# Pool groups of a hybrid decoder block: windows of 8 and 16 by a running sum, the window of 2 by one difference

## The chip, the cores and the metric

The kernel runs on one core of one Trainium2 chip. Time is device microseconds of one execution; before the change three runs took 1905.4, 1900.44 and 1904.27 us, a median of 1904.27. The profile is of one further execution. The engines are named as in the profile: PE is TensorE (PEld its weight loads), DVE is VectorE, ACT is ScalarE, POOL is GpSimd, SP is SyncE, which here issues most DMAs. Each engine works through its own queue in order; an instruction that has to wait holds up all that stand behind it on that engine.

## The reference

One decoder layer on 2048 tokens of 1024 features, all in float32:

```
h = x + W_out( concat[ RMSNorm(PoolMix(u_pool)), RMSNorm(StickBreakAttn(q, k, v)) ] )
    with [u_pool | q | k | v] = RMSNorm(x) @ W_in
h = h + W_down( relu(RMSNorm(h) @ W_up) ** 2 )
y = RMSNorm(h)
```

The change is in the pool mixer. It has four groups of 128 channels with windows of 2, 4, 8 and 16 tokens:

```python
for g, w in enumerate(POOL_WINDOWS):          # 2, 4, 8, 16
    xg = ug[:, :, g, :]
    cs = jnp.cumsum(xg, axis=1)
    cs_lag = jnp.pad(cs, ((0, 0), (w, 0), (0, 0)))[:, :S]
    count = jnp.minimum(pos + 1, w)
    outs.append((cs - cs_lag) / count - xg)   # mean of the last w tokens, less the token
mapped = jnp.einsum('bsgc,gcd->bsgd', pooled, pool_w)
y = mapped.reshape(B, S, D_POOL) * pool_scale
```

## The kernel before

Features lie on the 128 partitions and tokens along the free dimension, in four tiles of 512 tokens (j = 0 to 3). Every float32 product is made of three matmuls on a high and a low part: `split` (L145, L146) lets ACT copy the high part and DVE subtract it for the low part. That pair of lines serves the weights (`hl`), the normalized input (`h`), the attention tiles (`at`), the queries and keys (`qk`) and the pool tiles (`pls`).

The program has a front, an output projection, and two feed-forward stages. In the front the tiles go through the input projection in two pairs (0 and 1, then 2 and 3). A projection group is 24 matmuls (L177 to L179) into one of two PSUM banks, `pd`, and then an evacuation: `pool_group` for column groups 0 to 3, `keep_qk` and `keep_v` for the others. Weights are split `WAHEAD = 5` halves of a group ahead. Tiles 0 and 2 take their pool groups after six other groups, tile 1 takes them first and tile 3 last. In between, pieces of the attention are put in: logits `pz` (L630, L631), a scan of products on DVE (L663), transposes `pta` (L677), a split into `at`, and the products with the values, `po` (L689), summed at L648 (`ot`).

`pool_group(j, g, ps)` takes the projected group from PSUM into `u` (ACT L394, for tile 0 DVE L392), with the last `PAD` = 15 tokens of the tile before in front of it (POOL, L390 and L395). The sum over the window is made by doubling: at L400 an add of the tile to itself shifted by 1, then 2, 4 and 8 tokens, so one add for the window of 2 and four for that of 16. L403 makes `pl`, the sum times 1/w less `u`; in tile 0, L405 and L406 correct the first w - 1 tokens with a table of reciprocals. `pl` is split into `pls`, three matmuls with the pool's weights `pw` follow (L410 to L412, into `pp`), and ACT scales the result (L413). `pool_weights` loads these weights (L296) and splits them.

The order on each engine is set by a scheduler, which plans the whole program with estimated durations when the kernel is built. So a change of one stage's instructions also moves others against each other on all engines.

Of the kernel before, what the change touches and what calls it, by code (L numbers as in the profile page):

```python
# [8 lines left out]
F32 = mybir.dt.float32  # L9
# [4 lines left out]
ALU = mybir.AluOpType  # L14

P = 128
S = 2048
D = 1024
T = 512
NT = S // T  # L20
# [8 lines left out]
WARM = 9  # L29
SCRATCH = 2048  # L30
WINDOWS = (2, 4, 8, 16)
PAD = 15
EPS = 1e-6
RATIO_FRONT = (0.3, 0.4, 0.15, 0.4, 0.4, 0.3)
RATIO_TAIL = 0.6
# [10 lines left out]
def hymba_block(ctx: ExitStack, tc: tile.TileContext, xT, gains, w_in, pool_w, w_out, w_up, w_down, out):  # L46
    nc = tc.nc
# [3 lines left out]
    const = pool("const", 1)  # L51
# [55 lines left out]
    for n in (D, D // 2):  # L107
        inv[n] = const.tile([P, 1], F32, name=f"inv{n}")
        nc.vector.memset(inv[n], 1.0 / n)
    recip = const.tile([P, PAD], F32, name="recip")  # L110
    for i in range(PAD):
        nc.vector.memset(recip[:, i:i + 1], 1.0 / (i + 1))
# [9 lines left out]
    yrlast = const.tile([P, 2, 2, TB], F32R, name="yrlast")  # L122
    carry = const.tile([P, len(WINDOWS), PAD], F32, name="carry")
    nc.vector.memset(carry, 0.0)


    qs = [[dram.tile([P, T], F32R, name=f"qs{h}_{j}") for j in range(NT)] for h in range(H)]
# [14 lines left out]
    def split(dst, src):  # L142

        hi, lo = dst
        nc.scalar.activation(hi, src, AF.Copy)  # L145
        return nc.vector.tensor_tensor(lo, src, hi.bitcast(F32), ALU.subtract)  # L146
# [147 lines left out]
    def pool_weights():  # L294
        raw = pa.tile([P, PAD + T], F32, tag="s", name="pw_raw")[:, 0:4 * P].rearrange("p (g c) -> p g c", g=4)
        nc.sync.dma_start(raw, pool_w)  # L296
        pw.append(pa.tile([P, 2, 4, P], F32R, name="pw", bufs=1))
        split((pw[0][:, 0], pw[0][:, 1]), raw)

# [85 lines left out]
    def pool_group(j, g, ps):  # L385
        w = WINDOWS[g]
        if g == 0:
            st[j]["y"] = pa.tile([P, 4, T], F32, tag="yb", name="yb", bufs=1)
        u = pa.tile([P, PAD + T], F32, tag="u", name="u")
        nc.gpsimd.tensor_copy(u[:, 0:PAD], carry[:, g])  # L390
        if j == 0:
            took = nc.vector.tensor_tensor(u[:, PAD:], ps, st[0]["r"], ALU.mult)  # L392
        else:
            took = nc.scalar.activation(u[:, PAD:], ps, AF.Copy)  # L394
        nc.gpsimd.tensor_copy(carry[:, g], u[:, T:T + PAD])  # L395
        cur, lag = u, 1
        while lag < w:
            nxt = pa.tile([P, PAD + T], F32, tag="s", name="s")
            lo = 2 * lag - 1
            nc.vector.tensor_tensor(nxt[:, lo:], cur[:, lo:], cur[:, lo - lag:PAD + T - lag], ALU.add)  # L400
            cur, lag = nxt, 2 * lag
        pl = pa.tile([P, T], F32, tag="ev", name="pl")
        nc.vector.scalar_tensor_tensor(pl, cur[:, PAD:], 1.0 / w, u[:, PAD:], op0=ALU.mult, op1=ALU.subtract)  # L403
        if j == 0:
            nc.vector.tensor_tensor(pl[:, 0:w - 1], cur[:, PAD:PAD + w - 1], recip[:, 0:w - 1], ALU.mult)  # L405
            nc.vector.tensor_tensor(pl[:, 0:w - 1], pl[:, 0:w - 1], u[:, PAD:PAD + w - 1], ALU.subtract)  # L406
        d = pa.tile([P, 2, T], F32R, tag="st", name="pls", align_bytes=256, bufs=3)
        split((d[:, 0], d[:, 1]), pl)
        pp = psx.tile([P, T], F32, tag="px", name="pp")
        nc.tensor.matmul(pp, pw[0][:, 0, g], d[:, 0], start=True, stop=False)  # L410
        nc.tensor.matmul(pp, pw[0][:, 0, g], d[:, 1], start=False, stop=False)
        nc.tensor.matmul(pp, pw[0][:, 1, g], d[:, 0], start=False, stop=True)  # L412
        nc.scalar.activation(st[j]["y"][:, g], pp, AF.Copy, scale=gs[:, g:g + 1])  # L413
        return took
# [47 lines left out]
    def in_proj(j, c, again=False):  # L462
        if not again:
            wlist.append(w_in[c])
        if c < 4:
            evac = lambda ps: pool_group(j, c, ps)
        elif c < 12:
            evac = lambda ps: keep_qk(j, c % 4, qs if c < 8 else ks, ps)
        else:
            evac = lambda ps: keep_v(j, c - 12, ps)  # L470
# [37 lines left out]
    def front(q):  # L508
# [7 lines left out]
        if q == 0:  # L516
            note(start)
            note(norm1_first)
            note(pool_weights)
        else:  # L520
            note(lambda: (load_x(b, bigp), norm1_rms(b), norm1(b), pace(2)))
# [1072 lines left out]
    pa = inner.enter_context(tc.tile_pool(name="pa", bufs=2))  # L1594
# [70 lines left out]
```

## Time and profile before

| | |
|---|---|
| median of three runs | 1904.27 us (1900.44 to 1905.4) |
| the profiled execution | 1902.05 us, its span 1900.3 us |
| mean granted TensorE clock | 0.995 |
| instructions | 26640 |
| VectorE busy from 0 to 600 us | 477.48 us |
| TensorE busy from 0 to 600 us | 586.35 us |

The front and the output projection take about the first 600 to 700 us. A row of windows gives the busy time of each engine in a stretch and the TensorE clock that was granted there. A row of waits says which engine and line waited for which, how long in total, how often, and the longest. A row of the timeline has start, length, engine, line and operation, and in brackets how long the engine had stood idle and what ended that. Matmuls are pipelined: their lengths overlap, and what counts is the distance from start to start.

### The profile page before, as it was taken

What the parts mean: (1) busy time and instruction counts of PE and PEld (TensorE: products, weight loads), DVE (VectorE), ACT (ScalarE), POOL (GpSimd) and SP (SyncE); (2) the same over time, 40 slices, a digit from 0 to 9 for tenths busy, and PEclk for the clock granted to TensorE, in tenths of its full rate; (3) what the DMA queues carried; (4) which work ended last, traced back from release to release, by engine and by line L of the source; (5) the groups of instructions that cost most, each with busy time, mean ns of one, the idle gap of its engine ahead of it and who ended that gap; (6) DMA issues with size and microseconds to landing.
All of it is one profiled execution on the core that took longest, in us unless ns stands there. A gap on an engine that the chain in (4) does not pass through costs nothing.

```text
span 1900.3 us, 26640 instructions
## 1 busy us (share of the span) xinstructions
PE 1868.9 (98%) x8883; PEld 1554.3 (82%) x8883; DVE 1481.2 (78%) x2151; ACT 1025.2 (54%) x1616; POOL 238.5 (13%) x463
## 2 busy tenths in 40 slices
PE   9999999999999999999999999999999999999997
PEld 7788788788888888777888888887888888888886
DVE  6887789678866886778799988786666677988774
ACT  6565567455644465554567555554332665656543
POOL 0233234122321050000000000000010010020120
PEclk9999999999999999999999999999999999999998
DMA  7676596699888777787899888889999899999852
GB/s 226 212 255 201 177 313 224 194 322 315 281 310 312 278 252 254 284 303 274 307 358 328 303 308 281 298 284 333 388 313 330 281 317 307 332 294 341 289 206 91
DMA packets 222164, 535.91 MB, mean 282 GB/s; under 512 B 26048, under 2 KB 32192, under 8 KB 218176
## 3 DMA queue, kind: packets, MB, share of 16 engines
q1 hardware_dynamic: 217264, 525.46, 79.4%
q0 software_dynamic: 4608, 8.39, 2.4%
q8 instruction: 72, 1.18, 0.3%
q14 instruction: 76, 0.62, 0.1%
q10 hardware_dynamic: 144, 0.26, 0.0%
HBM read 349.46 MB, written 184.55 MB: 281 GB/s over the span
## 4 chain that ended last, share of the span: by engine, by line
PE 50%; DMA 5%; DVE 2%; issue 1%; ACT 1%; POOL 0%; SPq 0%; DVEq 0%; ACTq 0%
PE pb L1291 14%; PE pY L1118 13%; PE pb L1468 12%; PE pZ L1118 7%; PE pX L1118 3%; DMA ar<-sd 1%; DMA hn<-hs 1%; DMA ar<-sdi 1%; PE pb L1408 1%; DMA td<-t 0%; DMA t<-in_w_down_dram 0%; DMA b<-in_w_down_dram 0%; DMA wr<-in_w_down_dram 0%; DVE ad L146 0%; DVE hw L146 0%
## 5 line engine op out<-in xcount | busy, mean ns | idle before, releaser
L1118 PE MATMUL pY<-sa,hw 128*128 128x512 f32 x1536 | 366.3, 390 | 1.9 <-ACT u L1041 1.9
L1118 PEld LDWEIGHTS pY<-sa,hw 128*128 128x128 f32 x1536 | 287.9, 188 | 63.0 <-ACT u L1041 3.4
L1291 PE MATMUL pb<-ad,wd 128*128 128x512 f32 x1344 | 305.4, 389 | 0.7 <-DVE ad L146 0.7
L177 PE MATMUL pd<-h,hl 128*128 128x512 f32 x752 | 297.9, 396 | 1.5 <-DVE qk L146 1.3
L178 PE MATMUL pd<-h,hl 128*128 128x512 f32 x752 | 297.0, 395 | 0.3 <-DVE h L146 0.3
L179 PE MATMUL pd<-h,hl 128*128 128x512 f32 x752 | 297.3, 395 | 0.0
L1291 PEld LDWEIGHTS pb<-ad,wd 128*128 128x128 f32 x1344 | 252.1, 188 | 53.8 <-DVE ad L146 1.5
L1468 PE MATMUL pb<-ad,wd 128*128 128x512 f32 x1104 | 253.9, 390 | 0.9 <-ACT ad L145 0.9
L1468 PEld LDWEIGHTS pb<-ad,wd 128*128 128x128 f32 x1104 | 206.5, 188 | 44.6 <-ACT ad L145 1.3
L146 DVE TENSOR_TENSOR ad<-ar,ad 128x1024 fp32r<-128x1024 f32 x160 | 194.1, 1221 | 44.1 <-ACT ad L145 43.5
L145 ACT ACTIVATE ad<-ar 128x1024 fp32r<-128x1024 f32 x160 | 168.4, 1054 | 95.7 <-PE pb L1468 31.9
L1118 PE MATMUL pZ<-sa,hw 128*128 128x512 f32 x768 | 186.8, 390 | 1.7 <-DVE a L1061 1.7
L1118 PEld LDWEIGHTS pZ<-sa,hw 128*128 128x128 f32 x768 | 143.9, 188 | 32.7 <-DVE a L1061 3.0
L145 ACT ACTIVATE hl<-raw 128x512 fp32r<-128x512 f32 x168 | 104.1, 629 | 115.6 <-PE pd L179 76.7
L177 PEld LDWEIGHTS pd<-h,hl 128*128 128x128 f32 x752 | 142.2, 189 | 29.0 <-DVE qk L146 1.8
L179 PEld LDWEIGHTS pd<-h,hl 128*128 128x128 f32 x752 | 142.0, 189 | 28.2 <-DVE hl L146 0.5
L178 PEld LDWEIGHTS pd<-h,hl 128*128 128x128 f32 x752 | 142.2, 189 | 27.1 <-DVE h L146 0.7
L146 DVE TENSOR_TENSOR hl<-raw,hl 128x512 fp32r<-128x512 f32 x168 | 115.1, 690 | 46.9 <-ACT hl L145 46.5
L1035 ACT ACTIVATE a<-a 128x512 f32<-128x512 f32 x96 | 60.1, 629 | 89.6 <-DVE a L1077 38.5
L146 DVE TENSOR_TENSOR hw<-rt,hw 128x512 fp32r<-128x512 f32 x128 | 86.5, 686 | 25.2 <-ACT hw L145 25.1
L145 ACT ACTIVATE wd<-wq 128x1024 fp32r<-128x1024 f32 x56 | 59.4, 1060 | 77.1 <-PE pb L1291 68.4
L146 DVE TENSOR_TENSOR wd<-wq,wd 128x1024 fp32r<-128x1024 f32 x56 | 68.5, 1222 | 34.3 <-ACT wd L145 32.8
(218 smaller groups left out, 2737.3 us busy)
## 6 DMA issues: line engine op xcount, KB each, us to landing
ar<-sd SPq DMA_DIRECT2D x96, 512.0 KB, 5.9
ar<-sdi SPq DMA_DIRECT2D x64, 512.0 KB, 5.6
rb<-in_w_up_dram SPq DMA_DIRECT2D x30, 1024.0 KB, 6.2
sd<-a SPq DMA_DIRECT2D x104, 256.0 KB, 5.2
raw<-in_w_in_dram SPq DMA_DIRECT2D x50, 512.0 KB, 4.6
sdi<-hr SPq DMA_DIRECT2D x96, 256.0 KB, 5.4
wr<-in_w_down_dram SPq DMA_DIRECT2D x48, 512.0 KB, 5.7
sd<-s SPq DMA_DIRECT2D x88, 256.0 KB, 4.9
```

Of the source, the lines that this page charges most:

```text
L145: nc.scalar.activation(hi, src, AF.Copy)
L146: return nc.vector.tensor_tensor(lo, src, hi.bitcast(F32), ALU.subtract)
L177: nc.tensor.matmul(ps, hl[:, 0, c], hi, start=(k == 0), stop=False)
L178: nc.tensor.matmul(ps, hl[:, 0, c], lo, start=False, stop=False)
L179: last_mm[0] = nc.tensor.matmul(ps, hl[:, 1, c], hi, start=False, stop=(k == n - 1))
L1035: nc.scalar.activation(t, src, AF.Relu)
L1118: nc.tensor.matmul(t, w[:, wx, c], a[:, ax, c % 2], start=first and c == 0 and x == 0, stop=last and c == G - 1 and x == 2, skip_group_che ...
L1291: nc.tensor.matmul(b, t[:, wx, 2 * (kk % 2) + c, i * P:(i + 1) * P], a[:, ax, c], start=p in ("P1", "P5", "P2") and kk == 0 and c == 0 and ...
L1408: nc.tensor.matmul(b[:, cols], block(t, wx, c, n), a[:, ax, c, cols], start=False, stop=(i == 1 and c == 1 and x == 2), skip_group_check=True)
L1468: nc.tensor.matmul(ps[q, n], block(t, wx, c, n), left_[q][:, ax, c], start=(n_ in ("P1", "P3") and kk == 0 and c == 0 and x == 0), stop=(n ...
```

## The change

For the window of 2, `pl` becomes the token before less the token, one subtraction; the factor 1/2 is put on that group's weights when they are loaded (L299 of the changed kernel, before the split). The first token of the sequence is set to zero. For the window of 4 there are two adds as before, over fewer columns. For 8 and 16 one scan adds the incoming token and subtracts the one that leaves the window, starting from `window_sum`, the sum of the last w tokens of the tile before, which a reduce makes after the scan (not in the last tile). The padding becomes 16 tokens, so that the token leaving a window of 16 is at hand.

```diff
-PAD = 15
+PAD = 16
...
+    window_sum = const.tile([P, len(WINDOWS)], F32, name="window_sum")
+    nc.vector.memset(window_sum, 0.0)
...
         nc.sync.dma_start(raw, pool_w)
+        nc.vector.tensor_scalar(raw[:, 0], raw[:, 0], 1.0 / WINDOWS[0], None, op0=ALU.mult)
...
         nc.gpsimd.tensor_copy(carry[:, g], u[:, T:T + PAD])
-        cur, lag = u, 1
-        while lag < w:
-            nxt = pa.tile([P, PAD + T], F32, tag="s", name="s")
-            lo = 2 * lag - 1
-            nc.vector.tensor_tensor(nxt[:, lo:], cur[:, lo:], cur[:, lo - lag:PAD + T - lag], ALU.add)
-            cur, lag = nxt, 2 * lag
         pl = pa.tile([P, T], F32, tag="ev", name="pl")
-        nc.vector.scalar_tensor_tensor(pl, cur[:, PAD:], 1.0 / w, u[:, PAD:], op0=ALU.mult, op1=ALU.subtract)
-        if j == 0:
-            nc.vector.tensor_tensor(pl[:, 0:w - 1], cur[:, PAD:PAD + w - 1], recip[:, 0:w - 1], ALU.mult)
-            nc.vector.tensor_tensor(pl[:, 0:w - 1], pl[:, 0:w - 1], u[:, PAD:PAD + w - 1], ALU.subtract)
+        if w == 2:
+            nc.vector.tensor_tensor(pl, u[:, PAD - 1:PAD + T - 1], u[:, PAD:], ALU.subtract)
+            if j == 0:
+                nc.vector.tensor_tensor(pl[:, 0:1], u[:, PAD:PAD + 1], u[:, PAD:PAD + 1], ALU.subtract)
+        else:
+            sums = pa.tile([P, PAD + T], F32, tag="s", name="s")
+            if w == 4:
+                pair = pa.tile([P, PAD + T], F32, tag="s", name="s")
+                nc.vector.tensor_tensor(pair[:, PAD - 2:], u[:, PAD - 2:], u[:, PAD - 3:PAD + T - 1], ALU.add)
+                nc.vector.tensor_tensor(sums[:, PAD:], pair[:, PAD:], pair[:, PAD - 2:PAD + T - 2], ALU.add)
+            else:
+                nc.vector.tensor_tensor_scan(sums[:, PAD:], u[:, PAD:], u[:, PAD - w:PAD + T - w], window_sum[:, g:g + 1],
+                                             op0=ALU.add, op1=ALU.subtract)
+                if j < NT - 1:
+                    nc.vector.tensor_reduce(window_sum[:, g:g + 1], u[:, PAD + T - w:], axis=mybir.AxisListType.X, op=ALU.add)
+            nc.vector.scalar_tensor_tensor(pl, sums[:, PAD:], 1.0 / w, u[:, PAD:], op0=ALU.mult, op1=ALU.subtract)
...
```

In tile 0 the correction by reciprocals stays for the windows of 4, 8 and 16. The scheduler plans the program anew; the number and kind of PE's instructions stay the same, and from the end of the output projection on the order is the one of before on every engine.

Two places of the new order follow. Rows give the line, operation and operands. In the order a scan is printed as SCALAR_TENSOR_TENSOR. Line numbers are of the kernel that the rows belong to: L148 and L675 of the changed kernel are L146 and L663 of the one before.

The first is tile 1, DVE's queue up to the low part of `pls` of the window of 16. Before:

```order
L400 TENSOR_TENSOR s<-s 128x520
L146 TENSOR_TENSOR hl<-raw,hl 128x512
L663 SCALAR_TENSOR_TENSOR pc<-sh,later_keys 128x512
L648 TENSOR_TENSOR ot<-ot,po 64x512
L400 TENSOR_TENSOR s<-s 128x512
L672 TENSOR_TENSOR sg<-sg,pc 128x2x255
L740 TENSOR_SCALAR zero<-left_137 128x16
L146 TENSOR_TENSOR at<-pta,at 128x384
L146 TENSOR_TENSOR hl<-raw,hl 128x512
L403 SCALAR_TENSOR_TENSOR pl<-s,u 128x512
L741 TENSOR_REDUCE zall<-zero 128x1
L146 TENSOR_TENSOR pls<-pl,pls 128x512
```

The same place with the change:

```order
L660 TENSOR_TENSOR ot<-ot,po 64x512
L414 TENSOR_REDUCE window_sum<-u 128x1
L415 SCALAR_TENSOR_TENSOR pl<-s,u 128x512
L148 TENSOR_TENSOR h<-nt,h 128x512
L148 TENSOR_TENSOR at<-pta,at 128x512
L148 TENSOR_TENSOR h<-nt,h 128x512
L680 TENSOR_TENSOR sg<-sg,pc 128x127
L680 TENSOR_TENSOR sg<-sg,pc 128x255
L148 TENSOR_TENSOR hl<-raw,hl 128x512
L148 TENSOR_TENSOR h<-nt,h 128x512
L148 TENSOR_TENSOR pls<-pl,pls 128x512
```

The last scan of the attention's tile 0 (L663), its product `sg` of 2x255 and the `at` of 384 columns stood ahead of `pls` before; with the change they stand behind it.

On PE, the same pool group's first matmul (L410, with the change L422) stood behind the transposes of an attention unit. Before:

```order
L179 MATMUL pd<-h,hl 128x512
L677 MATMUL pta<-ident,sg 128x128 x3
L177 MATMUL pd<-h,hl 128x512
L178 MATMUL pd<-h,hl 128x512
L179 MATMUL pd<-h,hl 128x512
L410 MATMUL pp<-pls,pw 128x512
```

With the change:

```order
L701 MATMUL po<-at,vw 128x128
L422 MATMUL pp<-pls,pw 128x512
L643 MATMUL pz<-kw,qb 128x256
L642 MATMUL pz<-kw,qa 128x256
L701 MATMUL po<-at,vw 64x128
```

It has moved up, ahead of these transposes and into the products of an earlier unit.

The second place is tile 2, DVE's queue around the `pl` of the window of 16. Before:

```order
L146 TENSOR_TENSOR at<-pta,at 128x512
L400 TENSOR_TENSOR s<-s 128x520
L146 TENSOR_TENSOR hl<-raw,hl 128x512
L663 SCALAR_TENSOR_TENSOR pc<-sh,later_keys 128x512
L400 TENSOR_TENSOR s<-s 128x512
L672 TENSOR_TENSOR sg<-sg,pc 128x2x255
L146 TENSOR_TENSOR at<-pta,at 128x512
L403 SCALAR_TENSOR_TENSOR pl<-s,u 128x512
L648 TENSOR_TENSOR ot<-ot,po 64x512
```

With the change:

```order
L675 SCALAR_TENSOR_TENSOR pc<-sh,later_keys 128x512
L414 TENSOR_REDUCE window_sum<-u 128x1
L415 SCALAR_TENSOR_TENSOR pl<-s,u 128x512
L148 TENSOR_TENSOR pls<-pl,pls 128x512
L148 TENSOR_TENSOR at<-pta,at 128x512
L191 TENSOR_TENSOR ss<-ss,sq 128x512
L684 TENSOR_TENSOR sg<-sg,pc 128x2x255
L675 SCALAR_TENSOR_TENSOR pc<-sh,later_keys 128x512
L660 TENSOR_TENSOR ot<-ot,po 64x512
```

The adds between the attention's rows are gone, and `pl` has moved ahead of the `at` rows that follow it. In the start of the program, the row `L299 TENSOR_SCALAR pw_raw<-pw_raw 128x128` comes in between the last two `h` rows of the first tile on DVE.

More of the change, by code (lines that the diff above doesn't have):

```diff
@@ L395, in pool_group @@
         nc.gpsimd.tensor_copy(carry[:, g], u[:, T:T + PAD])
-        cur, lag = u, 1
-        while lag < w:
-            nxt = pa.tile([P, PAD + T], F32, tag="s", name="s")
-            lo = 2 * lag - 1
-            nc.vector.tensor_tensor(nxt[:, lo:], cur[:, lo:], cur[:, lo - lag:PAD + T - lag], ALU.add)
-            cur, lag = nxt, 2 * lag
-        pl = pa.tile([P, T], F32, tag="ev", name="pl")
-        nc.vector.scalar_tensor_tensor(pl, cur[:, PAD:], 1.0 / w, u[:, PAD:], op0=ALU.mult, op1=ALU.subtract)
-        if j == 0:
-            nc.vector.tensor_tensor(pl[:, 0:w - 1], cur[:, PAD:PAD + w - 1], recip[:, 0:w - 1], ALU.mult)
-            nc.vector.tensor_tensor(pl[:, 0:w - 1], pl[:, 0:w - 1], u[:, PAD:PAD + w - 1], ALU.subtract)
+        pl = pa.tile([P, T], F32, tag="ev", name="pl")
+        if w == 2:
[14 more added lines that the diff above has]
+            nc.vector.scalar_tensor_tensor(pl, sums[:, PAD:], 1.0 / w, u[:, PAD:], op0=ALU.mult, op1=ALU.subtract)
+            if j == 0:
+                nc.vector.tensor_tensor(pl[:, 0:w - 1], sums[:, PAD:PAD + w - 1], recip[:, 0:w - 1], ALU.mult)
+                nc.vector.tensor_tensor(pl[:, 0:w - 1], pl[:, 0:w - 1], u[:, PAD:PAD + w - 1], ALU.subtract)
         d = pa.tile([P, 2, T], F32R, tag="st", name="pls", align_bytes=256, bufs=3)
```

## The prediction

> **What bounds the kernel now.** First the engine table of the page:
>
> ```profile
> span 1900.3 us, 26640 instructions
> PE 1868.9 (98%) x8883; PEld 1554.3 (82%) x8883; DVE 1481.2 (78%) x2151; ACT 1025.2 (54%) x1616; POOL 238.5 (13%) x463
> ```
>
> TensorE (PE) is busy for all but 31 us. The change takes nothing from PE, so shorter VectorE (DVE) work is worth only what PE loses by waiting for it. The windows show where. Columns: window and length, then busy us (instructions) of PE, weight load, DVE, ACT and POOL, granted clock, DMA share, GB/s.
>
> ```profile
> 200.00:210.00 10.00, 6.36 (x38) 5.11 (x36) 9.62 (x19) 4.24 (x8) 4.84 (x3) 1.00 0.69 224
> 210.00:220.00 10.00, 9.43 (x34) 7.43 (x35) 5.79 (x10) 5.37 (x11) 0.00 (x0) 0.83 0.61 150
> 330.00:340.00 10.00, 7.83 (x48) 6.26 (x47) 10.00 (x16) 6.12 (x11) 6.46 (x4) 1.00 0.25 87
> 340.00:350.00 10.00, 9.34 (x38) 7.73 (x39) 8.29 (x13) 4.97 (x9) 0.79 (x3) 0.66 0.65 176
> 50.00:100.00 50.00, 48.99 (x236) 40.00 (x235) 44.41 (x81) 27.93 (x50) 11.42 (x27) 1.00 0.66 217
> 100.00:150.00 50.00, 48.70 (x294) 41.83 (x293) 43.46 (x69) 32.55 (x63) 19.09 (x33) 1.00 0.79 251
> ```
>
> Two places stand out, each a hole in PE followed by a lowered clock, with DVE full ahead of it. The list of waits (for whom: us, times, longest) and the timeline (start, length) say what PE waited for. Place A, token tile 1:
>
> ```profile
> PE pp L410 <- ACT pls L145: 4.0, 1, 4.0
> 205.97 0.40 PE L179 MATMUL pd<-h,hl 128*128 128x512 f32 x1
> 206.44 0.67 DVE L400 TENSOR_TENSOR s<-s 128x512 f32<-128x512 f32 x1
> 208.95 0.68 DVE L403 SCALAR_TENSOR_TENSOR pl<-s,u 128x512 f32<-128x512 f32 x1
> 209.66 0.63 ACT L145 ACTIVATE pls<-pl 128x512 fp32r<-128x512 f32 x1 [2.63 <-DVE pl L403]
> 210.35 0.50 PE L410 MATMUL pp<-pls,pw 128*128 128x512 f32 x1 [3.98 <-ACT pls L145]
> 212.09 0.63 PE L177 MATMUL pd<-h,hl 128*128 128x512 f32 x1
> 212.52 0.63 PE L178 MATMUL pd<-h,hl 128*128 128x512 f32 x1
> 214.47 0.40 PE L177 MATMUL pd<-h,hl 128*128 128x512 f32 x1
> 214.70 0.40 PE L178 MATMUL pd<-h,hl 128*128 128x512 f32 x1
> ```
>
> The pool matmul of the window of 16 stands in PE's queue for a `pl` that DVE makes only at 208.95, behind its fourth doubling add. Afterwards matmuls start 0.43 us apart (212.09, 212.52) instead of 0.23 (214.47, 214.70). Place B, tile 2:
>
> ```profile
> PE pta L677 <- DVE at L146: 1.9, 1, 1.9
> 337.95 0.65 DVE L400 TENSOR_TENSOR s<-s 128x512 f32<-128x512 f32 x1
> 339.14 0.67 DVE L146 TENSOR_TENSOR at<-pta,at 128x512 fp32r<-128x512 f32 x1
> 339.74 0.67 DVE L403 SCALAR_TENSOR_TENSOR pl<-s,u 128x512 f32<-128x512 f32 x1
> ```
>
> Here PE waits for an attention tile `at`, which stands in DVE's queue behind the doubling adds of the same pool group.
>
> **What the two places cost.** From the windows, hole plus clock: A is 10 - 6.36 = 3.64, 10 - 9.43 = 0.57 and (1 - 0.83) x 10 = 1.7, together 5.9 us. B is 2.17 + 0.66 + 3.4 = 6.2 us. Sum **12.1 us**.
>
> **The change part by part.** Prices of DVE operations, from the groups by line and shape (busy, mean ns):
>
> ```profile
> L400 DVE TENSOR_TENSOR s<-u 128x526 f32<-128x526 f32 x16 | 11.2, 697 | 3.6 <-ACT u L394 3.6
> L400 DVE TENSOR_TENSOR s<-s 128x524 f32<-128x524 f32 x12 | 8.3, 692 | 0.1
> L400 DVE TENSOR_TENSOR s<-s 128x520 f32<-128x520 f32 x8 | 5.5, 693 | 0.1
> L400 DVE TENSOR_TENSOR s<-s 128x512 f32<-128x512 f32 x4 | 2.7, 670 | 0.0
> L663 DVE TENSOR_TENSOR_SCAN pc<-sh,later_keys 128x512 f32<-128x512 f32 x56 | 68.6, 1226 | 0.7 <-ACT sh L636 0.7
> L741 DVE TENSOR_REDUCE zall<-zero 128x1 f32<-128x16 f32 x1 | 0.2, 158 | 0.0
> ```
>
> Window 2: add and scaled difference become one difference, 0.69 us less. Window 4: two adds stay, nothing. Window 8: three adds (2.08) become a scan and a small reduce (1.23 + 0.16), 0.69 less. Window 16: four adds (2.75) become the same pair, 1.36 less. That is 2.74 us a tile, 11 us over four tiles; tile 3 has no reduce (0.3 more), tile 0 loses one tiny operation. The scan of add and subtract on two f32 streams is not in the trace. Bounds: 0.69 (a plain add) and 2.45 (twice the nearest scan); I take the row, 1.23.
>
> [...]
>
> What matters more is where the rows now stand. At A, PE's queue holds 109 matmuls between the first pool matmul of window 4 and that of window 16 before, 87 now: with 0.227 us for 512 columns (214.70 - 214.47), half of it for 256, 0.085 for 128 and 0.12 for a transpose, 20.6 and 16.8 us, so PE asks 3.8 us earlier. In DVE's queue, between the second half of window 4's `pls` and the `pl` of window 16, stand 41 rows before (27.9 us) and 23 now (16.4 us), at 0.69 us a 512-wide operation, 0.75 for the six `nt`, 1.23 a scan, and less for narrower rows: ready 11.5 us earlier. The margin grows by 7.7 us and the wait is 4.0: it goes. At B the same count gives 119 against 90 matmuls (19.1, 15.4 us) and 26 against 13 DVE rows (20.0, 9.5 us), a margin better by 6.8 us; the `at` rows lose the adds ahead of them. Were the scan 2.45 us, 2.4 more would stand at each place and both waits would still go. What is late next: attention rows that the pool rows have passed at A (`at`, `sg`, the L663 scan). Each costs PE nothing as long as DVE, full from 190 to 210 before, has its 7.7 us.
>
> Added cost: the scaling of `pw_raw` enters DVE's queue between the third and the fourth of these four rows, and waits there for a DMA.
>
> ```profile
> 8.14 0.33 SPq L296 DMA_DIRECT2D pw_raw<-in_pool_w_dram  x1
> DMA to landing us min/median/max: 5.4/5.4/5.4
> 12.05 2.74 DVE L354 SCALAR_TENSOR_TENSOR h<-xt,gains,h 128x512 fp32r<-128x512 f32 x4
> 17.86 0.62 PE L482 MATMUL pd<-h,hl 128*128 128x512 f32 x2
> ```
>
> It lands at 13.5, DVE comes there at 14.1; the last `h` behind it is used only after 17.86, over 3 us of cover. Its own time, between 0.16 (the reduce) and 0.69 us (a 128x512 operation), is hidden there too; nothing is charged. If the load came over 4 us late, PE would stand for the excess.
>
> Sum against the profiled execution (1902.05 us): 1902.05 - 12.1 = 1890.0. That execution lies 2.2 below the median of the runs, 1904.27, which gives 1892.2 by the same step; I say **1891**.
>
> **The rivals.**
> *One stall stays, or half of each.* PE comes to B about 6 us earlier than before while DVE is still full there (10.00 of 10). Then some 6 us are gained: 1896 to 1898. The granted clock bears on this: B shows that single waits of 1.87 us, close together, already brought the clock down (0.66). [...]
>
> *No net change.* The pool matmuls were moved up with the sums; if the 23 DVE rows wait for inputs rather than run back to back, PE meets the same hole in another row: 1902 to 1904. Against it, DVE was 9.62 and 10.00 busy, so rows removed do count.
>
> *Slower.* The stage after (output projection) gets its weights just in time:
>
> ```profile
> ACT hl L145 <- DMA raw<-in_w_out_dram: 16.6, 6, 5.4
> ```
>
> Weights are split five halves ahead, 5 x 12 x 0.227 = 13.6 us of matmuls. A load is up to 5.4 late now, so 8.2 more can be borne. If those transfers do not move up when PE does (12.1 us), PE stands 3.9 us, the clock falls, and again at the next tiles: the gain is lost, and three bouts at 3.4 us (B) end at 1902 + 10.2 = 1912. It decides once loads land over 13.6 us late. Against: the loads are issued as buffers come free, which happens earlier too.
>
> **How the numbers follow.** Forecast 0.60, one stall left 0.17, no net change 0.14, slower 0.09. About 0.3% (5.7 us: below 1898.6 or above 1910.0) is what a measurement can tell from none. Faster: nearly all of the first and most of the second, 0.73; slower 0.08; same 0.19. Range: downward, the holes of 1.0 and 1.3 us at 50 to 150 may go too, and 1888 less some scatter (the runs span 5 us) is 1885; upward through the second rival to 1901, leaving out about 0.2.
>
> **What would show it.** Right: PE busy 10.00 and clock 1.00 in tile 1's and tile 2's pool stretch, no PE wait on `pls` over 1 us, a scan near 1.23 us, DVE about 11 us less busy. Wrong: another PE wait over 2 us with a clock under 1.00 between 50 and 600; a scan over 2.4 us; PE waiting on `hl` after 490.

## The result and the profile after

| | median us | lowest to highest | runs |
|---|---|---|---|
| before | 1902.41 | 1900.44 to 1905.4 | 4 |
| changed | 1888.08 | 1887.35 to 1889.65 | 4 |

The ratio is 0.9922, with an interval of 0.9909 to 0.9934: 14.3 us less. The profiled execution of the changed kernel took 1887.35 us, 14.7 below that of before; the spans differ by 14.8.

The page of the changed kernel begins so:

```profile
span 1885.5 us, 26640 instructions
PE 1862.9 (99%) x8883; PEld 1550.5 (82%) x8883; DVE 1472.8 (78%) x2135; ACT 1025.8 (54%) x1616; POOL 222.0 (12%) x463
```

Span less PE's busy time is PE's idle time: 31.4 us before, 22.6 now, 8.8 less. PE's busy time, with the same 8883 matmuls, is 6.0 us shorter, which is about the time that its lowered clock had cost (1.7 and 3.4 us at the two places). So the gain is all PE's, as idle time and as clock.

The windows of the changed kernel, with the columns of those of before (length, busy us and instructions of PE, weight load, DVE, ACT and POOL, granted clock, DMA share, GB/s):

```profile
50.00:100.00 50.00, 49.36 (x244) 41.01 (x243) 42.16 (x75) 28.03 (x50) 14.62 (x39) 1.00 0.69 228
100.00:150.00 50.00, 49.81 (x301) 42.54 (x299) 46.78 (x74) 32.51 (x63) 10.95 (x22) 1.00 0.81 265
200.00:210.00 10.00, 10.00 (x51) 8.39 (x50) 10.00 (x17) 6.01 (x12) 2.32 (x2) 1.00 0.85 256
210.00:220.00 10.00, 10.00 (x61) 8.67 (x59) 7.88 (x13) 6.20 (x11) 1.15 (x2) 1.00 0.75 236
320.00:330.00 10.00, 9.51 (x56) 7.81 (x55) 10.00 (x16) 7.91 (x14) 3.98 (x6) 1.00 0.43 107
330.00:340.00 10.00, 10.00 (x59) 8.59 (x58) 7.17 (x12) 3.39 (x7) 3.88 (x17) 1.00 0.79 266
340.00:350.00 10.00, 10.00 (x50) 8.44 (x49) 5.41 (x8) 3.25 (x6) 0.00 (x0) 1.00 0.81 248
```

Both holes are gone: PE is busy 10.00 of 10 in all four windows in which they lay, with the clock at 1.00. The kernel is ahead by now, so that the pool matmuls of B start at 325.5 us (343.2 before); the window in which they stand has 0.49 us of idle time left, also at full clock. DVE is still full at 200 to 210; PE does not wait for it there. In the list of PE's waits (for whom: us, times, longest) there is none on `pls` any more, and the longest wait on DVE in the attention is short:

```profile
PE pta L689 <- DVE sg L684: 0.9, 1, 0.9
```

For the whole front, the first 600 us, the windows say, before:

```profile
0.00:600.00 600.00, 586.35 (x3120) 492.26 (x3121) 477.48 (x768) 343.39 (x619) 155.77 (x326) 0.99 0.78 260
```

and after:

```profile
0.00:600.00 600.00, 594.20 (x3188) 500.11 (x3189) 478.94 (x768) 348.91 (x630) 144.44 (x342) 1.00 0.78 265
```

PE is idle 13.65 us before and 5.80 after, 7.85 less; the clock lost 1.7 at 210 to 220 and 3.4 at 340 to 350 before and nothing after. That is 12.95 of the 14.8 us. Counted by rows it is more. PE's 3236th matmul is the first from which on its rows are the same in both kernels. Before it starts at 623.05 us, in the changed kernel at 608.90:

```profile
623.05 0.39 PE L177 MATMUL pd<-h,hl 128*128 128x512 f32 x1
608.90 0.39 PE L179 MATMUL pd<-h,hl 128*128 128x512 f32 x1
```

So 14.15 of the 14.8 us are gained ahead of this row. The 1.2 us between 12.95 and 14.15 are neither in the idle time nor in the clock of these windows. DVE's busy time up to 600 us is about the same in both, because the changed kernel has got further by then (3188 matmuls for 3120).

### The profile page after: what moved, and what is told of

Read it like the earlier page. It is cut to its first block, busy times and chain, and to the rows that moved or that the text cites. A ratio compares the mean times of both kernels' runs of the same rounds, so it can differ in the third digit from the quotient of the medians.

```text
span 1885.5 us, 26640 instructions
## 1 busy us (share of the span) xinstructions
PE 1862.9 (99%) x8883; PEld 1550.5 (82%) x8883; DVE 1472.8 (78%) x2135; ACT 1025.8 (54%) x1616; POOL 222.0 (12%) x463
## 4 chain that ended last, share of the span: by engine, by line
PE 52%; DMA 3%; DVE 2%; ACT 1%; issue 1%; POOL 0%; SPq 0%; DVEq 0%; ACTq 0%
PE pb L1303 16%; PE pY L1130 13%; PE pb L1480 12%; PE pZ L1130 7%; PE pX L1130 3%; DMA hn<-hs 1%; PE pb L1420 1%; DMA td<-t 0%; DMA sdi<-a 0%; DMA b<-in_w_down_dram 0%; DMA ar<-sd 0%; DMA t<-in_w_down_dram 0%; DVE hw L148 0%; DMA sd<-a 0%; ACT a L1047 0%
## 5 line engine op out<-in xcount | busy, mean ns | idle before, releaser
L148 DVE TENSOR_TENSOR ad<-ar,ad 128x1024 fp32r<-128x1024 f32 x160 | 194.1, 1221 | 41.6 <-ACT ad L147 41.1
L147 ACT ACTIVATE ad<-ar 128x1024 fp32r<-128x1024 f32 x160 | 168.9, 1057 | 90.0 <-PE pb L1480 31.9
L179 PEld LDWEIGHTS pd<-h,hl 128*128 128x128 f32 x752 | 141.5, 188 | 27.7 <-DVE qk L148 0.7
L181 PEld LDWEIGHTS pd<-h,hl 128*128 128x128 f32 x752 | 141.4, 188 | 27.6
L147 ACT ACTIVATE hl<-raw 128x512 fp32r<-128x512 f32 x168 | 104.5, 630 | 103.0 <-PE pd L181 71.3
L148 DVE TENSOR_TENSOR hl<-raw,hl 128x512 fp32r<-128x512 f32 x168 | 115.3, 691 | 47.3 <-ACT hl L147 47.3
L148 DVE TENSOR_TENSOR hw<-rt,hw 128x512 fp32r<-128x512 f32 x128 | 86.5, 685 | 25.3 <-ACT hw L147 25.2
L147 ACT ACTIVATE wd<-wq 128x1024 fp32r<-128x1024 f32 x56 | 59.5, 1063 | 79.7 <-PE pb L1303 69.2
L148 DVE TENSOR_TENSOR wd<-wq,wd 128x1024 fp32r<-128x1024 f32 x56 | 68.5, 1223 | 35.9 <-ACT wd L147 35.8
```

The source lines that it names most:

```text
L179: nc.tensor.matmul(ps, hl[:, 0, c], hi, start=(k == 0), stop=False)
L181: last_mm[0] = nc.tensor.matmul(ps, hl[:, 1, c], hi, start=False, stop=(k == n - 1))
```

## The experiments

All kernels compute the whole of the reference. "Below" is against the kernel before on the same chip, by the ratio of the runs. Line numbers are those of the kernel that a row belongs to: they shift by some ten lines.

| kernel | median us | before, us | ratio | interval |
|---|---|---|---|---|
| e1_scan_only | 1890.49 | 1903.29 | 0.9929 | 0.9908 to 0.9951 |
| e2_diff_only | 1902.06 | 1903.29 | 0.9986 | 0.9972 to 1.0 |
| e3_pad_only | 1903.46 | 1903.29 | 1.0 | 0.9988 to 1.0013 |
| e4_scan_twice | 1894.96 | 1903.29 | 0.9959 | 0.9945 to 0.9973 |
| e5_tile1 | 1898.74 | 1902.77 | 0.9972 | 0.996 to 0.9984 |
| e6_tile2 | 1898.12 | 1902.77 | 0.997 | 0.9959 to 0.9981 |
| e7_tiles12 | 1892.47 | 1905.09 | 0.9927 | 0.9912 to 0.9942 |
| e8_tiles03 | 1900.7 | 1905.09 | 0.9977 | 0.9965 to 0.9989 |
| e9_put_off | 1906.62 | 1905.09 | 1.0018 | 1.0004 to 1.0033 |

The theory is the prediction's: two waits of PE for a backlogged DVE, A in tile 1 and B in tile 2, and the lowered clock behind each, go. The main rival is load: DVE simply has some 11 us less to do, and the time follows it wherever it was.

### Which part of the change does it: the scan, the difference or the padding

The scan alone (against the changed kernel: window 2 by doubling again, and no scaling of the weights):

```diff
-        nc.vector.tensor_scalar(raw[:, 0], raw[:, 0], 1.0 / WINDOWS[0], None, op0=ALU.mult)
...
-        if w == 2:
+        if False:
...
+            if w == 2:
+                sums, lag = u, 1
+                while lag < w:
...
```

> Windows 8 and 16 by the running sum in all tiles, window 2 by doubling as before, its weights unscaled. Theory one, the two stalls: the gain is what TensorE lost by waiting at place A (tile 1) and place B (tile 2) and by the lowered clock behind each, so whatever empties VectorE's queue there by more than the waits (4.0 and 1.9 us) gives all of it. Here: both go, 12 to 14 us below the kernel before, no wait on pls or at over 1 us, clock 1.00. Theory two, the load: the gain goes with the VectorE time taken out, 8.4 of 11.1 us here, so about 10.8 of the 14.3 us.

The difference alone (against the changed kernel: windows 4, 8 and 16 by doubling):

```diff
-            sums = pa.tile([P, PAD + T], F32, tag="s", name="s")
-            if w == 4:
+            if w > 2:
+                sums, lag = u, 1
+                while lag < w:
...
```

> Window 2 by one difference with the half in the weights, windows 4, 8 and 16 by doubling as before. The two stalls: the pool matmuls of the window of 16 stand at the same place of TensorE's queue in tile 1 as before (and 4 rows earlier in tile 2), VectorE has 0.69 us less ahead of them, so a wait of about 3.3 us with a lowered clock stays at A, and B stays too: 0 to 3 us below the kernel before. The load: 2.7 of 11.1 us taken out, 3.5 us below. The two do not differ much here; the trace must tell whether the holes are still there.

The padding alone (against the kernel before):

```diff
-PAD = 15
+PAD = 16
```

> The kernel before with 16 instead of 15 tokens of padding, nothing else; the planned order of TensorE's queue is that of before, row for row. Both theories: no difference (within 0.15%), both holes there, each with its lowered clock. If it were some us faster, the padding or the placement in memory that follows from it would be a cause of its own.

Measured: the scan alone is 13.5 us below (0.0071 x 1903.29), the difference alone 2.7 below with an interval that reaches to no change, the padding alone 0. The interval of the scan alone, 9.3 to 17.5 us, holds what both theories said (12 to 14, and 10.8), so it does not part them. Its windows show A closed:

```profile
200.00:210.00 10.00, 10.00 (x54) 8.47 (x53) 10.00 (x18) 6.44 (x12) 2.32 (x2) 1.00 0.83 251
210.00:220.00 10.00, 10.00 (x58) 8.60 (x57) 8.37 (x13) 6.20 (x11) 1.14 (x2) 1.00 0.74 240
```

At B it has 0.70 us of idle time, at 320 to 330, and none from 330 to 350.

With the difference alone both waits are still there. The columns are for whom, us in total, times, longest; L432 and L699 are L410 and L677 of the kernel before, and L147 and L148 are its L145 and L146:

```profile
PE pp L432 <- ACT pls L147: 3.4, 1, 3.4
PE pta L699 <- DVE at L148: 2.0, 1, 2.0
```

So the scans for 8 and 16 carry nearly all of it. The padding moves no row of PE's queue, and PE's two waits are 4.0 and 1.9 us, as before.

### Which tile: one stall at a time

The scan is used in the tiles named, with doubling for 8 and 16 in the others and for the window of 2 in all; the reduce that hands on the last sums stays only in the tile ahead of a scan. For tile 1, against the changed kernel:

```diff
+            if w == 2 or w > 4 and j not in (1,):
+                sums, lag = u, 1
+                while lag < w:
...
+            if w == 2 or w > 4 and j not in (1,):
+                if w > 4 and j == 0:
+                    nc.vector.tensor_reduce(window_sum[:, g:g + 1], u[:, PAD + T - w:], axis=mybir.AxisListType.X, op=ALU.add)
...
-                if j < NT - 1:
+                if False:
```

> The running sum for windows 8 and 16 in tile 1 alone (tile 0 makes the two window sums), all else by doubling as before. The two stalls: A goes, B stays: about 6 us below the kernel before (5 to 7), clock 1.00 around 200 to 220 us and below 1.00 around 340. The load: 1.7 us of VectorE time taken out of 11.1, so about 2 us below.

The same with `(2,)`, and the reduce in tile 1:

> The running sum for windows 8 and 16 in tile 2 alone (tile 1 makes the two window sums), all else by doubling as before. The two stalls: B goes, A stays: about 6 us below the kernel before (5 to 7), clock below 1.00 around 210 us and 1.00 around 340. The load: 1.7 us taken out of 11.1, so about 2 us below.

Measured: 5.3 us below with tile 1 alone, 5.7 with tile 2 alone. In the windows of the first, A is closed and B is open:

```profile
200.00:210.00 10.00, 10.00 (x55) 8.53 (x54) 9.97 (x18) 7.41 (x14) 2.16 (x3) 1.00 0.73 200
210.00:220.00 10.00, 10.00 (x54) 8.55 (x53) 8.94 (x16) 5.61 (x10) 1.71 (x3) 1.00 0.76 252
330.00:340.00 10.00, 7.47 (x42) 6.00 (x41) 9.94 (x16) 7.56 (x14) 1.78 (x3) 0.84 0.55 166
340.00:350.00 10.00, 10.00 (x49) 8.34 (x49) 4.55 (x8) 1.68 (x3) 0.60 (x4) 0.99 0.75 196
```

In those of the second, A is open and B is closed but for 0.68 us:

```profile
200.00:210.00 10.00, 8.90 (x49) 7.20 (x47) 9.91 (x17) 4.56 (x9) 4.32 (x2) 1.00 0.54 178
210.00:220.00 10.00, 6.95 (x17) 5.25 (x18) 7.35 (x14) 3.96 (x8) 0.66 (x2) 0.66 0.65 177
330.00:340.00 10.00, 9.32 (x52) 6.80 (x51) 10.00 (x15) 7.22 (x15) 3.52 (x5) 1.00 0.67 248
340.00:350.00 10.00, 10.00 (x64) 8.46 (x63) 9.73 (x14) 5.97 (x12) 1.19 (x4) 1.00 0.83 246
```

Each stall goes with the scan of its own tile, and each is worth about what its term said (5.9 and 6.2 us). The 2 us of the load theory lie outside both intervals (3.0 to 7.6 and 3.6 to 7.8 us). Then both tiles together, and the other two tiles together, by the same edit with `(1, 2)` and `(0, 3)`:

> The running sum for windows 8 and 16 in tiles 1 and 2 only, tiles 0 and 3 and the window of 2 by doubling as before. The two stalls: A and B both go, 11 to 13 us below the kernel before, with clock 1.00 in both places, though only 3.8 of the 11.1 us of VectorE time are taken out. The load: 3.8 of 11.1 is a third, about 5 us below.

> The running sum for windows 8 and 16 in tiles 0 and 3 only, tiles 1 and 2 and the window of 2 by doubling as before. The two stalls: both stay, 0 to 1 us below the kernel before, from the small holes at 70 to 120 us. The load: 4.2 of the 11.1 us are taken out, about 5 us below.

Measured: tiles 1 and 2 give 13.9 us, as much as the whole change within the intervals, with half of its scans; the load theory's 5 us are far below the interval of 11.0 to 16.8. PE is busy 10.00 of 10 from 200 to 220 and from 330 to 350, at full clock, with 0.65 us of idle time at 320 to 330. Tiles 0 and 3 give 4.4 us. With these two both waits stand, as the list of PE's waits says:

```profile
PE pp L432 <- ACT pls L147: 4.0, 1, 4.0
PE pta L699 <- DVE at L148: 2.1, 1, 2.1
```

and the windows show A (10 - 5.99) and B (10 - 6.98) no narrower than before, each with a lowered clock:

```profile
200.00:210.00 10.00, 5.99 (x26) 4.30 (x25) 9.30 (x17) 5.13 (x10) 4.84 (x3) 0.87 0.72 241
...
330.00:340.00 10.00, 6.98 (x44) 5.92 (x45) 9.94 (x16) 6.50 (x12) 1.59 (x3) 0.85 0.40 133
```

That the same removal is worth three times as much in the two tiles with the stalls as in the two without speaks for the stalls. The 4.4 us are more than the theory of two stalls allowed (0 to 1), and here the load theory came nearer (about 5). Part of it has a place: the small holes of tile 0. From 50 to 150 us PE is busy 99.7 of 100 us with tiles 0 and 3, for 97.7 before. In all seven kernels with doubling in tile 0 it is 97.3 to 97.8, and in the four with the scan there 98.4 to 99.7. Idle time and clock loss of the front are 16.8 us against 18.7 before, so 1.9 of the 4.4 can be pointed to, in one profiled execution. The rest stays open; it may be scatter, as the interval reaches from 2.1 to 6.7 us.

### Is it the work taken from DVE, or where it stands

Against the changed kernel, every scan is done twice, into the same tile:

```diff
+                for _ in range(2):
+                    nc.vector.tensor_tensor_scan(sums[:, PAD:], u[:, PAD:], u[:, PAD - w:PAD + T - w], window_sum[:, g:g + 1],
+                                                 op0=ALU.add, op1=ALU.subtract)
```

> The changed kernel with each of the eight running sums made twice into the same tile: 8 x 1.24 = 9.9 us of VectorE time come back, nearly all that the change takes out, while TensorE's planned queue keeps the pool matmuls where they stand in the kernel with only the running sums. The two stalls: at A VectorE's 16.4 us between the windows of 4 and 16 become 18.9 against 16.8 us of matmuls, still 5.3 us better than before where 4.0 were short; at B 12.0 against 15.4. So both stay away and the time is 11 to 14 us below the kernel before. The load: 1.2 us taken out in all, so 1 to 2 us below.

Measured: 7.8 us below, with an interval of 5.1 to 10.5. This lies between what the two theories said (11 to 14, and 1 to 2), and both missed. The page's DVE row and the group of the scan (times, busy us, mean ns, idle before it):

```profile
PE 1864.6 (99%) x8883; PEld 1550.0 (82%) x8883; DVE 1481.4 (78%) x2143; ACT 1026.9 (54%) x1616; POOL 227.8 (12%) x463
```

```profile
L412 DVE TENSOR_TENSOR_SCAN s<-u,window_sum 128x512 f32<-128x512 f32 x16 | 20.4, 1274 | 0.3 <-ACT u L397 0.2
```

DVE does as much as before the change (1481.4 against 1481.2 us), and yet the kernel is faster by more than half of the gain. So the load as a whole does not set the time. What is left of the holes:

```profile
200.00:210.00 10.00, 8.45 (x46) 6.58 (x45) 9.99 (x19) 7.03 (x13) 3.19 (x3) 1.00 0.74 239
210.00:220.00 10.00, 10.00 (x54) 8.57 (x53) 9.21 (x16) 5.60 (x10) 1.09 (x2) 1.00 0.64 193
330.00:340.00 10.00, 9.46 (x62) 7.92 (x59) 9.70 (x16) 9.06 (x17) 2.12 (x4) 1.00 0.72 213
340.00:350.00 10.00, 10.00 (x54) 8.53 (x54) 5.14 (x9) 3.06 (x6) 3.13 (x16) 1.00 0.79 222
```

At A there are 1.55 us of idle time again, while the clock stays at 1.00. B is 0.54 us, with 0.49 ahead of it at 320 to 330, as in the changed kernel. The expectation took PE's queue to keep the rows of the kernel with the scan alone. It didn't: the scheduler planned anew, and at A there are 109 matmuls (20.6 us) again between the pool groups of 4 and 16, as before. DVE's rows between the two groups take 20.4 us by the trace, for 24.7 before. So `pl` comes 4.3 us nearer, which is enough for the wait of 4.0, and the first pool matmul (L423) does not wait. What waits is the second one (L424), which needs the low part of `pls` from DVE:

```profile
203.04 0.68 DVE L416 SCALAR_TENSOR_TENSOR pl<-s,u 128x512 f32<-128x512 f32 x1
203.64 1.28 DVE L148 TENSOR_TENSOR hl<-raw,hl 128x512 fp32r<-128x512 f32 x2
204.84 1.21 DVE L676 TENSOR_TENSOR_SCAN pc<-sh,later_keys 128x512 f32<-128x512 f32 x1
205.97 0.66 DVE L148 TENSOR_TENSOR pls<-pl,pls 128x512 fp32r<-128x512 f32 x1
204.75 0.40 PE L423 MATMUL pp<-pls,pw 128*128 128x512 f32 x1
206.69 0.50 PE L424 MATMUL pp<-pls,pw 128*128 128x512 f32 x1 [1.55 <-DVE pls L148]
```

The new plan put three rows between `pl` and that low part, which starts 2.9 us after `pl`; before it started 1.4 us after it (208.95 and 210.33).

### Is it the row that waits, or the backlog behind it

Against the kernel before, only the pool matmuls of tile 1's window of 16, for which PE waits 4.0 us at A, are put off, by 77 rows (15 us) of PE's queue:

```diff
+        while put_off and put_off[0][0] <= 0:
+            with tc.issue_after(last_mm[0].ins):
+                put_off.pop(0)[1]()
...
+        if (j, g) == (1, 3):
+            put_off.append([3, mapped])
+        else:
+            mapped()
```

> The kernel before, where the three pool matmuls of the window of 16 in tile 1, those that TensorE waited 4.0 us for at A, are put 77 rows later in TensorE's queue (15 us of matmuls); VectorE's work is the same. First reading, a wait of one row: if only these matmuls were early, the hole at A goes and with it about 6 us, and B stays. Second reading, VectorE behind as a whole: in the trace of before the next group starts 0.6 us of matmuls behind these rows and needs the low part of qk, which VectorE ends at 211.6 us; so TensorE stands from 206 to about 211.5 all the same, now for qk, and the time is that of before within 1.5 us.

Measured: 3.4 us above, with an interval of 0.8 to 6.3. The wait on `pls` is gone, and PE stands in another row. The timeline (start, length; in the brackets the wait and for whom):

```profile
211.33 0.68 DVE L146 TENSOR_TENSOR qk<-pd,qk 128x512 fp32r<-128x512 f32 x1
212.07 0.79 PE L177 MATMUL pd<-h,hl 128*128 128x512 f32 x1 [5.31 <-DVE qk L146]
```

```profile
200.00:210.00 10.00, 6.76 (x39) 5.42 (x38) 9.92 (x19) 3.91 (x7) 4.64 (x2) 1.00 0.74 244
210.00:220.00 10.00, 7.93 (x28) 6.46 (x29) 5.81 (x11) 4.64 (x9) 0.20 (x1) 0.83 0.55 120
```

PE's next projection group goes into the bank `pd`, out of which DVE has yet to take the low part of `qk` of an earlier group, and that row stands in the same backlogged queue. To take one wait off PE's path is worth nothing there, for the next row of PE needs DVE too. The second reading had this wait right; its time, that of before within 1.5 us, was too low by the median. What the change did was different: with it DVE has fewer rows in the queue ahead of all of these.

## Why the prediction held, step by step

- **What bounds the kernel**, two holes with a lowered clock behind them: shown. Each goes with the scan of its own tile and stays without it, and the two tiles together bring the whole gain within the intervals.
- **The price of the scan.** The groups of the changed kernel by line and shape give it, with the other new rows:

```profile
L411 DVE TENSOR_TENSOR_SCAN s<-u,window_sum 128x512 f32<-128x512 f32 x8 | 10.2, 1275 | 0.2 <-ACT u L397 0.2
L414 DVE TENSOR_REDUCE window_sum<-u 128x1 f32<-128x16 f32 x3 | 0.5, 154 | 0.0
L299 DVE TENSOR_SCALAR pw_raw<-pw_raw 128x128 f32<-128x128 f32 x1 | 0.2, 223 | 0.0
L675 DVE TENSOR_TENSOR_SCAN pc<-sh,later_keys 128x512 f32<-128x512 f32 x56 | 69.3, 1239 | 3.9 <-ACT sh L648 3.9
```

  The nearest row, 1.23, was right to 0.05 us; the reduce was 0.15 against 0.16. The scan's 1275 ns against 684 to 697 for one of the pool's plain adds is 1.8 to 1.9 times. The pool's rows took 38.5 us of DVE before (the four groups of adds, 27.7, and the 16 `pl` of L403, 10.8). Now they take 27.6: 10.2 for the scans, 1.0 for the reduces, 0.2 for the scaling, 8.1 for the 12 `pl` of sums, and 8.1 for the window of 2 and the two adds of the window of 4. That is the 11 us forecast. On DVE's busy total only 8.4 appear, mostly because its rows overlap: in the rows of the doubled scan above, `hl` starts 0.60 us after `pl`, which is 0.68 long, and busy time counts the overlap once. Summed by length, all rows of DVE went from 1614.5 to 1604.1 us, 10.4 less; the other rows grew by 0.7, which is what the 56 scans of the attention did alone (68.6 to 69.3 us).
- **The margins.** +7.7 us at A and +6.8 at B were forecast, against waits of 4.0 and 1.9. Both waits are gone, but the margins were smaller. The count priced DVE's rows by their length (0.69), and they start 0.60 apart. By the traces the rows that were counted take 24.7 us before and 14.5 now at A, and 17.1 and 7.7 at B: 10.2 and 9.4 us less, which with PE asking 3.8 and 3.7 earlier leaves 6.4 and 5.7. Most of this is not the work taken out. Of the 10.2 us at A the pool's own rows give 1.8 (5.0 and now 3.2), less than the wait, and of the 9.4 at B 2.3; the rest are rows of `h`, `hl`, `at`, `sg` and the attention's scans that the new plan put at other places. No kernel has the new rows in the old order, so what the order does by itself is not shown. In the changed kernel the pool matmul of window 16 that needs the low part of `pls` stands at 203.46 us, without a wait, behind a `pls` of 200.47:

```profile
200.47 0.69 DVE L148 TENSOR_TENSOR pls<-pl,pls 128x512 fp32r<-128x512 f32 x1
203.46 0.40 PE L423 MATMUL pp<-pls,pw 128*128 128x512 f32 x1
```

- **The clock.** The sum counted 5.1 us of lowered clock, and none is left in the front. The kernels show what it did after each wait. At A it fell after waits of 3.4 to 5.3 us every time, to between 0.66 and 0.87 in a window (before, and in five of the experiments); after 1.5 us (the doubled scan) it stayed at 1.00. At B it fell after waits of 1.9 to 2.1 us in five kernels of six, to between 0.66 and 0.84. Wherever it was lowered, the loss was about 1.7 or 3.4 us, summed over the windows, and not by the length of the wait. The kernel with the padding alone has PE's order of before and its waits, and lost 3.4 us at A and 1.7 at B, the reverse of before:

```profile
210.00:220.00 10.00, 8.68 (x26) 6.70 (x27) 6.40 (x12) 4.48 (x8) 0.20 (x1) 0.66 0.47 114
340.00:350.00 10.00, 7.50 (x35) 6.38 (x36) 9.94 (x16) 5.55 (x11) 1.97 (x4) 0.83 0.64 184
```

  With the difference alone, after 2.0 us at B, it was 1.00:

```profile
330.00:340.00 10.00, 7.88 (x53) 6.63 (x52) 9.94 (x16) 6.27 (x12) 3.37 (x4) 1.00 0.30 93
340.00:350.00 10.00, 10.00 (x52) 8.18 (x51) 7.54 (x12) 4.20 (x8) 1.10 (x2) 1.00 0.78 207
```

  So A's 1.7 and B's 3.4 us of clock are prices of that execution, not fixed ones. These runs show no fixed length of a wait from which on the clock falls: it fell after 3.4 us and more at A each time, and after 1.9 at B (before, with waits of 0.3 and 0.7 us near it), but not after 2.0 there with the difference alone.
- **What is late next.** The attention rows that the pool's have passed cost PE nothing over 0.3 us: at A (195 to 230 us) the list shows no wait of PE, at B (320 to 352) two, of 0.3 and 0.2. The `sg` wait of 0.9 above lies at 410 to 420.
- **The scaling of the pool's weights.** It ran at 14.08 between the third and the fourth `h`, as the order and the load's landing said, for 0.22 us, and no row behind it waited:

```profile
14.08 0.22 DVE L299 TENSOR_SCALAR pw_raw<-pw_raw 128x128 f32<-128x128 f32 x1
14.22 0.75 DVE L357 SCALAR_TENSOR_TENSOR h<-xt,gains,h 128x512 fp32r<-128x512 f32 x1
```

- **The size, 12.1 us forecast and 14.3 measured.** The term that was too small is the one left out: the small holes. PE is busy 0.37 us more at 50 to 100 and 1.11 more at 100 to 150, 1.5 together, which the prediction had only in its low end. They go with the scans of tile 0, as the kernels with and without these show. Other holes came and went (0.51 and 0.49 us in two windows of the new kernel), so that idle time and clock give 12.95. By rows the front gave 14.15; the 0.6 us left of the spans lie where PE's order is the same, and no experiment ties them to the change.
- **Where a step failed.** "Were the scan 2.45 us, 2.4 more would stand at each place and both waits would still go." With the scan done twice (2 x 1.27) B went, and A had a wait of 1.5 us. The wait on `pl` did go, even with PE's pool matmul back in its old place. The new wait was for the low part of `pls`, which the step did not count: it added the time to the queues as the change had left them and stopped at `pl`, but a longer row makes the scheduler plan anew, and that plan put three rows behind `pl`. The margin of one order can't be carried over to another.
- **The rivals.** Neither one stall left, nor a hole in another row, nor late weights of the output projection came. The second of them did come in the kernel that only put the matmuls off: there PE met the same backlog in its next row.

## What to carry to other kernels

Where an engine is 98% busy, look for the windows in which it is not, and for the granted clock behind them; then count what stands in both queues between two fixed rows, for the engine that waits and for the one it waits for, by the distance of their starts and up to the last row that is waited for. Work taken from the other engine, with the plan that follows from it, pays where its queue is behind, and less elsewhere: two tiles of four brought nearly all of it (13.9 us of 14.3), and the same total of DVE work, otherwise placed, took 7.8 us less. Moving the row that waits was no cure for a queue that was late as a whole (3.4 us above the kernel before, with a wait of 5.3 in the next row), and a margin must be counted again for each new plan of the scheduler.

## What was not expected of the hardware

A wait of PE of about 2 us did not act on its clock alike: in the same place of nearly the same program the clock fell to 0.66 (before, a wait of 1.9), to 0.84 (scan in tile 1 alone, 1.9) and not at all (the difference alone, 2.0). Where it fell, it cost about 1.7 or 3.4 us at either place, and the same order of PE had the two the other way round in another kernel (the padding alone). What decides it was not tried.
